# RWKV's short products in pairs: heads on rows or columns of the array, parities alternating

## The chip, the cores and the metric

The kernel runs on one core of a Trainium2 chip. The metric is the device time of one execution in microseconds, the median over several runs. A profile is one further execution, taken with the hardware profiler; its own time stands beside its span in the table below.

The engines are named as the profile names them: PE multiplies matrices (PEld is its loading of the stationary operand, the weights), DVE is the vector engine, ACT the scalar engine, POOL the general one, SP issues most transfers. PE writes to PSUM, which has eight banks; a tile of 128 partitions by 512 float32 fills one bank. DVE and ACT read the results out of it.

## The reference, cut to what matters

One decoder layer: a norm, one input projection, three mixers side by side (latent attention, RWKV-7, gated linear attention), a gated merge and an output projection, for 2048 tokens of width 1024. The change touches RWKV-7 alone, 8 heads of width 64:

```
def step(state, inp):
    r_t, w_t, k_t, v_t, kk_t, a_t = inp
    sa = jnp.einsum('bhvk,bhk->bhv', state, -kk_t)
    state = (state * w_t[:, :, None, :] + sa[..., None] * (kk_t * a_t)[:, :, None, :]
             + v_t[..., None] * k_t[:, :, None, :])
    return state, jnp.einsum('bhvk,bhk->bhv', state, r_t)
```

Each head has a 64 x 64 state that decays, is corrected and is read once a token. The kernel works it out in chunks of 64 tokens: inside a chunk the token-by-token dependence becomes a triangular system, and only the state passes from chunk to chunk. Decay and learning rate come from two low-rank products (`tanh(lw) @ w_up`, `la @ a_up`), each with an inner width of 64.

## The kernel before, in words

`phase_rwkv` walks 2048 tokens in four blocks of 512 (TB). For each block and each of two groups `g` of four heads (two pairs `q`, each pair with heads `hd` 0 and 1 on partitions 0-63 and 64-127), it projects r, k and v with weights split in two parts (`mm3`, L130-L135: three products of 128 x 128 weights by 512 tokens). Every projection product is full size; these are the "fill" below. A block-and-group is done as two halves `u` of 256 tokens, that is 16 pieces `i`, and a piece has four chunks `cc` of 64 tokens: `j = cc // 2`, parity `e_ = cc % 2`.

A piece goes through five steps, whose products are short:

- `operands` (L627) makes the scaled vectors `ar` (128 columns a chunk: 64 of r, 64 of a) and `bk` (64 of k, 64 of b), and the decays. Its two low-rank products (`tanh_up`, L645) use a `wup` that is padded with zeros to 128 rows, so that one half of the input is ignored.
- `within` (L408) makes the scores inside a chunk. `arb` is a block-diagonal copy of `ar` (head 0 in one half, head 1 in the other, zeros elsewhere; copied by POOL at L416 and ACT at L417), so that one product of 128 x 128 by 256 (L423) gives both heads. DVE masks the result into `ma` and `mr` (L426, L427).
- `inverses` and `whole` solve the triangular systems: DVE on 32 x 32 blocks, then 32 products of 32 x 32 in L478 and 32 in L488 for each two pieces, first all of one parity, then all of the other.
- `prepare` (L496) turns `bk` and makes `rv`: 16 products of 64 x 64 (L515), again one parity after the other.
- `chain` (L523) runs the four chunks one after another. The state of both heads of a pair is a block-diagonal 128 x 128 matrix `Zb` (its scales `scm` and `s0m` are masked by head on POOL). For each chunk: read the state (L556, two products of 128 x 128 by 128), add `rv` on DVE (L561), four products of 64 x 64 with the inverse (L565), copy to `uv` on ACT (L569), two products of 128 x 128 by 128 for the update (L575), add and scale on DVE (L580, L530). The output of the chunk before is read with four products of 128 rows by 64 columns (L547) and added on DVE (L549).

The program is not written in the order in which it runs: a scheduler lays out each engine's instructions beforehand, by priorities (`high_priority`) and its own model of durations, and each engine then runs its list in order. `place` ties the first product of each chain step to a point among the fill products, spread evenly over the piece. RWKV has these PSUM banks: one for each of `psm` (within), `ps1`, `psq`, `psa`, `psu`, `psz` and two for the projections.

After RWKV come the attention, the gated linear attention and the merge; they are untouched in the source. `[128*64]` in a profile row means 128 rows and 64 columns of the array. A float32 product stands in the profile as two passes, so counts there are twice the number of products in the source.

## Time and profile before

| what | value |
|---|---|
| median of 3 runs | 3022.0 us (3018.12 to 3023.85) |
| the profiled execution's own time | 3010.5 us |
| its span, first to last instruction | 3008.7 us |
| mean granted clock of PE | 0.989 |
| PE busy | 2908.3 us, 97% of the span |
| DVE, ACT, POOL busy | 59%, 50%, 49% |
| last RWKV short product starts | 1231.8 us |

A row of a group reads: line, engine, operation, what it writes and reads, shape and count, then busy time and the mean length of one in ns, then the idle time just before it and who ended it. A matmul's length includes its way through the array, and the next one starts before it ends; what one costs in a stream is the distance from start to start.

### The profile page before, as it was taken

The page shows a single profiled execution, that of the slowest core. Times are in us where ns is not written, and L with a number is a line of the kernel's source. Part 1 is how long each engine was busy: PE and PEld are TensorE (multiplying, and loading weights), DVE is VectorE, ACT ScalarE, POOL GpSimd, SP SyncE. Part 2 cuts the span into 40 slices and gives each one's busy share as a digit, 9 for nine tenths or more (in the row PEclk, how much of TensorE's full clock was granted, in tenths as well). Part 3 has the DMA queues.
Part 4 walks back from the last instruction along what each step waited for, and adds up shares of the span by engine and source line. Part 5 has one row for each costly group of instructions (what it writes and reads, how often), then busy time and mean ns, then how long its engine had stood idle before and what let it go on. Part 6 is the DMA issues. An engine that isn't in the chain of part 4 may idle for free. (4 is left out here: it accounts for less than half of the span.)

```text
span 3008.7 us, 52742 instructions
## 1 busy us (share of the span) xinstructions
PE 2908.3 (97%) x17728; PEld 2395.9 (80%) x17728; DVE 1761.0 (59%) x4677; ACT 1503.9 (50%) x3463; POOL 1474.7 (49%) x1945
## 2 busy tenths in 40 slices
PE   7998999999999999999999999999999999999998
PEld 6776777777777878789999887788788888778887
DVE  3558675667746544388888886744324312975443
ACT  4444434454444436577877775554334434554221
POOL 4644544454444435555544555776334424575322
PEclk9999999999999999999999999999999999999999
DMA  4333323323233334300000014444223226866422
GB/s 135 105 100 103 90 85 101 93 77 86 78 106 86 106 112 144 113 20 22 19 20 16 15 62 148 148 143 136 92 96 101 92 91 203 288 201 212 137 97 78
DMA packets 285184, 312.67 MB, mean 104 GB/s; under 512 B 77920, under 2 KB 234608, under 8 KB 284912
## 3 DMA queue, kind: packets, MB, share of 16 engines
q1 hardware_dynamic: 259088, 278.76, 29.3%
q10 hardware_dynamic: 25824, 30.54, 3.1%
q8 instruction: 140, 2.29, 0.3%
q14 instruction: 132, 1.08, 0.1%
HBM read 233.16 MB, written 76.02 MB: 103 GB/s over the span
## 5 line engine op out<-in xcount | busy, mean ns | idle before, releaser
L119 POOL TENSOR_TENSOR w_lo<-w_raw,w_hi 128x256 fp32r<-128x256 f32 x848 | 645.0, 768 | 818.9 <-ACT w_hi L118 770.6
L133 PE MATMUL psd<-hh,w_hi 128*128 128x512 f32 x1952 | 795.1, 408 | 10.7 <-ACT w_hi L118 4.2
L135 PE MATMUL psd<-hh,w_lo 128*128 128x512 f32 x1952 | 788.4, 406 | 9.2 <-POOL w_lo L119 8.7
L134 PE MATMUL psd<-hl,w_hi 128*128 128x512 f32 x1952 | 778.3, 399 | 0.0
L118 ACT CAST w_hi<-w_raw 128x256 fp32r<-128x256 f32 x848 | 336.4, 404 | 501.8 <-PE psd L134 281.9
L135 PEld LDWEIGHTS psd<-hh,w_lo 128*128 128x128 f32 x1952 | 371.4, 190 | 95.5 <-POOL w_lo L119 17.9
L133 PEld LDWEIGHTS psd<-hh,w_hi 128*128 128x128 f32 x1952 | 371.2, 190 | 91.7 <-issue 8.9
L134 PEld LDWEIGHTS psd<-hl,w_hi 128*128 128x128 f32 x1952 | 371.1, 190 | 74.8 <-issue 1.2
L1286 POOL TENSOR_SCALAR P<-P,nm 128x1024 f32<-128x1024 f32 (+2 forms) x192 | 166.1, 875 | 192.5 <-DVE nm L1283 144.6
L1306 DVE TENSOR_TENSOR tl<-pst,th 128x512 fp32r<-128x512 f32 (+2 forms) x352 | 193.4, 562 | 33.6 <-ACT th L1305 32.0
L1305 ACT CAST th<-pst 128x512 fp32r<-128x512 f32 (+2 forms) x352 | 165.2, 488 | 81.6 <-PE pst L1301 42.5
L1278 ACT ACTIVATE P<-P,nm 128x1024 f32<-128x1024 f32 (+2 forms) x192 | 172.3, 901 | 14.8 <-DVE nm L1274 14.5
L1264 DVE TENSOR_SCALAR_CACHE_REDUCE P<-pss 128x512 f32<-128x512 f32 (+3 forms) x288 | 168.2, 593 | 13.1 <-PE pss L135 9.5
L1301 PE MATMUL pst<-cs,P 128*128 128x128 f32 x1088 | 166.0, 274 | 0.0
L1323 PE MATMUL pso<-th,v 128*128 128x256 f32 x576 | 150.9, 284 | 2.6 <-DVE yo L1331 2.6
L1323 PE MATMUL pso<-tl,v 128*64 128x256 f32 x576 | 139.9, 282 | 0.7 <-DVE tl L1306 0.7
L1301 PEld LDWEIGHTS pst<-cs,P 128*128 128x128 f32 x1088 | 125.6, 141 | 9.1 <-DVE tl L1306 0.4
L133 PE MATMUL pss<-kh,qh 128*128 128x512 f32 (+2 forms) x320 | 128.7, 402 | 0.6 <-DVE mx L1268 0.2
L119 POOL TENSOR_TENSOR wb_lo<-wb_raw,wb_hi 128x256 fp32r<-128x256 f32 x96 | 87.8, 921 | 80.6 <-ACT wb_hi L118 65.4
L1323 PEld LDWEIGHTS pso<-th,v 128*128 128x128 f32 x576 | 108.8, 189 | 11.8 <-DVE yo L1331 2.8
L135 PE MATMUL pss<-kh,ql 128*128 128x512 f32 (+2 forms) x320 | 116.4, 365 | 0.6 <-POOL ql L1244 0.6
L134 PE MATMUL pss<-kl,qh 128*128 128x512 f32 (+2 forms) x320 | 116.3, 364 | 0.0
(403 smaller groups left out, 5925.2 us busy)
## 6 DMA issues: line engine op xcount, KB each, us to landing
w_raw<-in_w_gate_dram SPq DMA_DIRECT2D x448, 128.0 KB, 2.2
pre<-plain SPq DMA_DIRECT2D x144, 256.0 KB, 2.3
w_raw<-in_w_rwkv_dram SPq DMA_DIRECT2D x208, 128.0 KB, 2.2
w_raw<-in_w_more_dram SPq DMA_DIRECT2D x192, 128.0 KB, 2.2
h_g<-pre SPq DMA_DIRECT2D x48, 512.0 KB, 4.4
h_x<-in_x_dram SPq DMA_DIRECT2D x44, 512.0 KB, 4.5
more<-plain SPq DMA_DIRECT2D x48, 256.0 KB, 2.7
wb_raw<-in_w_br_dram ACTq DMA_DIRECT2D x96, 128.0 KB, 3.5
```

Of the source, the lines that this page charges most:

```text
L118: nc.scalar.copy(hi, src)
L119: (sub or nc.gpsimd).tensor_tensor(out=lo, in0=src, in1=hi.bitcast(F32), op=ALU.subtract)
L133: mm(out, lhsT=lhs[0], rhs=rhs[0], start=start, stop=False)
L134: mm(out, lhsT=lhs[0], rhs=rhs[1], start=False, stop=False)
L135: m = mm(out, lhsT=lhs[1], rhs=rhs[0], start=False, stop=stop)
L1264: nc.vector.tensor_scalar(out=pt[:, c0:c0 + f], in0=s_[:, 0:f], scalar1=-MLA_SCALE, scalar2=3e38, op0=ALU.mult, op1=ALU.min, accum_out=mx[ ...
L1278: nc.scalar.activation(out=pt[:, cw], in_=pt[:, cw], func=AF.Exp, bias=nm[:, 0:1], scale=-1.0, accum_out=nm[:, 1 + n:2 + n])
L1286: nc.gpsimd.tensor_scalar(out=pt[:, cw], in0=pt[:, cw], scalar1=nm[:, 1:2], scalar2=1.0, op0=ALU.mult, op1=ALU.mult)
L1301: nc.tensor.transpose(tp[:, kl, qt, :], P[qt][:, kt * 128:(kt + 1) * 128], k.ident)
L1305: nc.scalar.copy(flat(th)[:, r], flat(tp)[:, r])
L1306: nc.vector.tensor_tensor(out=flat(tl)[:, r], in0=flat(tp)[:, r], in1=flat(th)[:, r].bitcast(F32), op=ALU.subtract)
L1323: nc.tensor.matmul(d_, lhsT=l_, rhs=r_, start=kt == 0 and j == 0, stop=last and kl == 1 and j == 1)
```

## The change

The five steps compute the same, but no longer through block-diagonal copies. Each product that took both heads at once, with zeros in half of its operand, becomes two products that use a part of the array each, issued one right after the other:

- by rows (64 rows, 128 columns; head 0 on partitions 0-63, head 1 on 64-127, results to two different banks): the scores of `within` (L418 in the new numbering), the state read (L542), the two low-rank products (L639, now before both tanh).
- by columns (128 rows, 64 columns; results to partitions 0-63 and 64-127): the state update (L561) and the output read (L574), which is now done once for two chunks, both parities in turn.
- the products with the inverse (L551) stay 64 x 64, but the two heads go to different columns of the same rows. ACT copies the result in two halves instead of one.
- parities alternate product by product in L477, L487 (32 x 32) and L514 (64 x 64).

Gone are `arb` and its copies, `scm`, `s0m`, the zeros of `wup`. The state is 64 wide rather than 128, so DVE's add and scale handle half the elements. `psm` takes two banks, and `psa`, `psu`, `psz` are one two-bank tile `cz` that is made once. `psm` also takes the low-rank products and no longer helps in the first transposition.

```diff
-        ps_a = pool("rw_psa", 1, space=PSUM)
-        ps_u = pool("rw_psu", 1, space=PSUM)
-        ps_z = pool("rw_psz", 1, space=PSUM)
+        ps_c = pool("rw_psc", 1, space=PSUM)
...
+        cz = ps_c.tile([128, 2, 512], F32, name="psc")
+        pA = cz[:, :, 0:128].rearrange("p h (q v) -> p q h v", q=2)
+        pU, pZ, pY = cz[:, 0, 128:256], cz[:, 0, 384:512].rearrange("p (q v) -> p q v", q=2), cz[:, 1, 128:384]
...
             for q in range(2):
-                nc.gpsimd.tensor_copy(arb[0:64, :, 0, :], ar[0:64, q])
-                nc.scalar.copy(arb[64:128, :, 1, :], ar[64:128, q])
+                pm = ps_m.tile([128, 2, 512], F32, name="psm")
+                pv = pm.rearrange("p h (e j t) -> p e j h t", e=2, j=2)
+                for e_ in range(2):
+                    for j in range(2):
+                        for hd, hs in heads:
+                            nc.tensor.matmul(pv[:, e_, j, hd], lhsT=bk[hs, q, 2 * j + e_, :], rhs=ar[hs, q, 2 * j + e_, :],
+                                             start=True, stop=True)
...
-            for e_, (lo_, up_) in enumerate(half_):
-                for u in range(2):
-                    for n_ in range(8):
+            for u in range(2):
+                for n_ in range(8):
+                    for e_, (lo_, up_) in enumerate(half_):
                         m = nc.tensor.matmul(ph[up_, u, n_, :], lhsT=mas[u][lo_, e_, n_, 32:64], rhs=xh[lo_, u, n_, :],
...
-                for q in range(2):
-                    m = nc.tensor.matmul(pA[:, q * 128:(q + 1) * 128], lhsT=ar[:, q, cc, :], rhs=Zb[:, q, :],
-                                         start=True, stop=True)
...
+                    for hd, hs in heads:
+                        m = nc.tensor.matmul(pA[:, q, hd], lhsT=ar[hs, q, cc, :], rhs=Z[hs, q, :], start=True, stop=True)
...
+                for q in range(2):
+                    for hd, osl in enumerate((asl, rsl)):
+                        hc = slice((2 * q + hd) * 64, (2 * q + hd) * 64 + 64)
+                        m = nc.tensor.matmul(pU[osl, q * 64:q * 64 + 64], lhsT=T[asl, idx(q, hd, j), :], rhs=rhs[asl, hc],
+                                             start=True, stop=True)
...
+                for hd, osl in enumerate((asl, rsl)):
+                    nc.scalar.copy(by_head(uv[:, j, e_, :])[asl, :, hd], pU[osl].rearrange("p (q v) -> p q v", q=2))
...
+                        m = nc.tensor.matmul(pZ[hs, q, :], lhsT=bkt[:, q, cc, hs], rhs=uv[:, j, e_, hc],
+                                             start=True, stop=True)
...
+                if e_:
+
+                    for hn in range(4):
+                        hc = slice(hn * 64, hn * 64 + 64)
+                        for x in range(2):
+                            nc.tensor.matmul(pY[halves(x)[1], hc], lhsT=mr[:, x, idx(hn // 2, hn % 2, j), :],
+                                             rhs=uv[:, j, x, hc], start=True, stop=True)
+                    nc.vector.tensor_tensor(out=ysb[:, j, :], in0=pY, in1=ysb[:, j, :], op=ALU.add)
...
+            pw = ps_m.tile([128, 2, 512], F32, name="psm")
+            for q, p in enumerate(P2):
+                for r_, rs_ in heads:
+                    nc.tensor.matmul(pw[:, r_, q * 256:q * 256 + 256], lhsT=wup[rs_, p * 128:(p + 1) * 128],
+                                     rhs=lwla[rs_, ts_], start=True, stop=True)
```

Where the short products stand in PE's list follows from the scheduler. This is PE before, in the middle of the RWKV stage (L645 low-rank, L565 inverse, L423 scores, L547 output read; L133 to L135 and L601 are full-size fill and transposes):

```order
L645 MATMUL ps_8168<-lwla,wup 128x256 x2
L134 MATMUL psd_8754<-hl_8072,w_hi 128x512
...
L601 MATMUL psq<-cs,ysb 128x128 x4
L565 MATMUL psu<-rhs,tt_161 64x64 x4
L423 MATMUL psm<-arb,bk_7673 128x256 x2
L645 MATMUL ps_8194<-lwla,wup 128x256 x2
L547 MATMUL psu<-uv_6265,mr_6752 64x64 x4
```

Only the runs of L565 and L547 use a part of the array here; L423 and L645 use all of it, like the fill. This is PE of the change, at a place with the same kinds (L561 update, L514 `rv`, L418 scores, L542 state read):

```order
L135 MATMUL psd_11143<-hh_8054,w_lo 128x512
L561 MATMUL psc<-uv_8147,bkt 64x64 x4
L514 MATMUL psq<-uv_9167,ma_9955 64x64 x16
L418 MATMUL psm<-ar_10852,bk_10853 128x128 x5
L542 MATMUL psc<-z_149,ar_8144 128x64 x4
L418 MATMUL psm<-ar_10852,bk_10853 128x128 x3
L133 MATMUL psd_11195<-hh_8040,w_hi 128x512
```

Between the two fill products every run is now on a part of the array: 128 x 64, then 64 x 64, then 64 x 128 three times. The scores are eight half products instead of four runs of two, and another step's four stand inside them.

The low-rank products (L639) are issued as four in a row in most pieces, but not in all of them. PE of the change, in an early piece:

```order
L616 MATMUL ps_3306<-cs,sq 128x2
L639 MATMUL psm<-lwla,wup 128x256
L135 MATMUL psd_3141<-hh_2202,w_lo 128x512
L133 MATMUL psd_3141<-hh_2204,w_hi 128x512
...
L134 MATMUL psd_3196<-hl_2195,w_hi 128x512
L639 MATMUL psm<-lwla,wup 128x256
L135 MATMUL psd_3196<-hh_2194,w_lo 128x512
```

Here two products of a pair stand apart, each alone among full-size ones. Of the 64 low-rank products nine stand alone so; forty stand in runs of four. Counted over the whole list, the stretches of PE's list with one shape of the array are 361 before and 613 now.

More of the change, by code (lines that the diff above doesn't have):

```diff
@@ L376, in phase_rwkv @@
             nc.gpsimd.memset(tt[i], 0.0)
-        arb = per.tile([128, 4, 2, 128], F32, name="arb")
-        nc.gpsimd.memset(arb, 0.0)
         ones2 = k.c("ones2", 128)
@@ L560, in chain @@
                 rhs = t3.tile([128, 256], F32, name="rhs")
-                nc.vector.tensor_tensor(out=rhs[asl], in0=pA[asl], in1=rv[asl, j, :], op=ALU.add)
-                pU = ps_u.tile([128, 2, 256], F32, name="psu")
-                for hn in range(4):
-                    hc = slice(hn * 64, hn * 64 + 64)
-                    m = nc.tensor.matmul(pU[asl, 0, hc], lhsT=T[asl, idx(hn // 2, hn % 2, j), :], rhs=rhs[asl, hc],
-                                         start=True, stop=True)
-                    if hn == 0:
-                        at(m, 3 * cc + 1)
@@ L569, in chain @@
-                nc.scalar.copy(uv[asl, j, e_, :], pU[asl, 0])
-                nc.scalar.copy(ysb[rsl, j, :], pA[rsl])
-                if cc:
-                    read(cc - 1, pU)
-                pZ = ps_z.tile([128, 2, 128], F32, name="psz")
-                for q in range(2):
-                    m = nc.tensor.matmul(pZ[:, q, :], lhsT=bkt[:, q, cc, :], rhs=uv[:, j, e_, q * 128:(q + 1) * 128],
-                                         start=True, stop=True)
-                    if q == 0:
-                        at(m, 3 * cc + 2)
@@ L579, in chain @@
-                zt = t3.tile([128, 2, 128], F32, name="zt") if cc < 3 else Zb
-                nc.vector.tensor_tensor(out=zt, in0=pZ, in1=Zb, op=ALU.add)
-                if cc < 3:
-                    scaled(zt, scm[:, :, cc])
-            read(3, ps_u.tile([128, 2, 256], F32, name="psu"))
+                nc.vector.tensor_tensor(out=by_head(rhs)[asl], in0=pA[asl], in1=by_head(rv[:, j, :])[asl], op=ALU.add)
+                for q in range(2):
+                    for hd, osl in enumerate((asl, rsl)):
+                        hc = slice((2 * q + hd) * 64, (2 * q + hd) * 64 + 64)
+                        m = nc.tensor.matmul(pU[osl, q * 64:q * 64 + 64], lhsT=T[asl, idx(q, hd, j), :], rhs=rhs[asl, hc],
+                                             start=True, stop=True)
+                        if q == hd == 0:
+                            at(m, 3 * cc + 1)
@@ new lines, in chain @@
+                zt = t3.tile([128, 2, 64], F32, name="zt") if cc < 3 else Z
+                nc.vector.tensor_tensor(out=zt, in0=pZ, in1=Z, op=ALU.add)
+                if cc < 3:
+                    scaled(zt, sc[:, :, cc:cc + 1])
+                if e_:
+                    for hn in range(4):
+                        hc = slice(hn * 64, hn * 64 + 64)
+                        for x in range(2):
+                            nc.tensor.matmul(pY[halves(x)[1], hc], lhsT=mr[:, x, idx(hn // 2, hn % 2, j), :],
+                                             rhs=uv[:, j, x, hc], start=True, stop=True)
+                    nc.vector.tensor_tensor(out=ysb[:, j, :], in0=pY, in1=ysb[:, j, :], op=ALU.add)
@@ L640, in operands, with tanh_up @@
             P2 = (2 * g, 2 * g + 1)
[L642 to L650 removed]
+            pw = ps_m.tile([128, 2, 512], F32, name="psm")
[3 more added lines that the diff above has]
+                                     rhs=lwla[rs_, ts_], start=True, stop=True)
+            def tanh_up(r_):
+                o = t1.tile([128, 2, 256], F32, name="ta", bufs=2)
+                for q, p in enumerate(P2):
+                    nc.scalar.activation(out=o[:, q, :], in_=pw[:, r_, q * 256:q * 256 + 256], func=AF.Tanh,
+                                         bias=half[:, 4 * r_ + p:4 * r_ + p + 1], scale=0.5)
                 return o
[L654 removed]
+            ta, tb = tanh_up(0), tanh_up(1)
             ld = t1.tile([128, 8, 65], F32, name="ld")
@@ L734, in operands @@
                 nc.scalar.copy(uv[es, :, e_, :], pv[es].rearrange("p j q t -> p j (q t)"))
[L735 removed]
+            return dict(B=B, g=g, u=u, ar=ar, bk=bk, bv=bv, uv=uv, sc=sc, s0=s0)
         n = 4 * NB
@@ L811, in phase_rwkv @@
         k.more_constants()
-        wup = t1.tile([128, 2, 512], F32, name="wup")
-        nc.gpsimd.memset(wup, 0.0)
-        for r_ in range(2):
-            rows_ = slice(64 * r_, 64 * r_ + 64)
-            nc.scalar.dma_start(out=wup[rows_, r_], in_=w_up2[rows_])
-        blk["h"] = turned(xs, (pl.ps[1], "psd1"), (ps_1, "ps1"), (ps_m, "psm"), (ps_q, "psq"))
+        wup = t1.tile([128, 512], F32, name="wup")
+        nc.scalar.dma_start(out=wup, in_=w_up2)
+        blk["h"] = turned(xs, (pl.ps[1], "psd1"), (ps_1, "ps1"), (ps_q, "psq"))
         project_group(0)
```

91 lines of the change are left out of this document (29 added, 62 removed).

## The prediction

> **What bounds the kernel now.** I read the page first, then the stretches of the program, then PE's waits, then PE's timeline inside the RWKV stage.
>
> ```profile
> PE 2908.3 (97%) x17728; PEld 2395.9 (80%) x17728; DVE 1761.0 (59%) x4677; ACT 1503.9 (50%) x3463; POOL 1474.7 (49%) x1945
> ```
> ```profile
> 0.00:1235.00 1235.00, 1172.38 (x7334) 938.14 (x7335) 732.23 (x1902) 578.57 (x1377) 599.15 (x849) 0.98 0.34 101
> 1235.00:2000.00 765.00, 748.46 (x4971) 653.99 (x4971) 577.82 (x1889) 531.15 (x1226) 423.95 (x536) 0.99 0.19 60
> ```
> ```profile
> L547 PE MATMUL psu<-uv,mr x512: 221/222/368, 217.3 to 1231.8; 128*64 128x64 f32 x171
> ```
> ```profile
> PE psd L223 <- DVE h_x L202: 13.4, 2, 11.0
> PE psa L556 <- DVE zbd L530: 8.4, 7, 3.3
> PE psz L575 <- ACT uv L569: 2.5, 1, 2.5
> ```
>
> PE is busy for 97%, no other engine for more than 59%. The RWKV stage runs to 1235 us (its last short product starts at 1231.8), and PE works for 1172 of these. Its waits there are small: 13.4 us at the start, 8.4 us in all for the scaled state, 2.5 us for `uv`. So the stage takes what PE's list takes, and the change is to be priced on PE; DVE at 732, ACT at 579 and POOL at 599 us of 1235 have room. These are the short products, by group (two passes each; busy, mean ns of one):
>
> ```profile
> L423 PE MATMUL psm<-arb,bk 128*128 128x256 f32 x256 | 68.7, 388 | 0.4 <-DVE bk L715 0.4
> L547 PE MATMUL psu<-uv,mr 128*64 128x64 f32 x512 | 46.0, 230 | 0.0
> L575 PE MATMUL psz<-uv,bkt 128*128 128x128 f32 x256 | 45.4, 300 | 2.5 <-ACT uv L569 2.5
> L565 PE MATMUL psu<-rhs,tt 64*64 64x64 f32 x512 | 44.2, 225 | 2.7 <-DVE rhs L561 2.6
> L556 PE MATMUL psa<-zbd,ar 128*128 128x128 f32 x256 | 43.5, 294 | 10.8 <-DVE zbd L530 8.4 <-DVE gn_t L166 2.4
> L645 PE MATMUL ps<-lwla,wup 128*128 128x256 f32 x128 | 33.9, 387 | 0.7 <-ACT ta L649 0.4 <-DVE kl_v L161 0.3
> L515 PE MATMUL psq<-uv,ma 64*64 64x64 f32 x512 | 32.4, 222 | 0.4 <-ACT bkt L506 0.4
> L488 PE MATMUL psq<-tt,xt 32*32 32x32 f32 x512 | 19.0, 192 | 0.0
> L478 PE MATMUL psq<-xt,ma 32*32 32x32 f32 x512 | 18.9, 195 | 3.3 <-DVE xt L474 3.3
> ```
>
> Their lengths overlap, so I price a pass by its distance from start to start. Timeline rows (start, length of the run, count):
>
> ```profile
> 564.31 0.40 PE L135 MATMUL psd<-hh,w_lo 128*128 128x512 f32 x1
> 564.63 0.68 PE L565 MATMUL psu<-rhs,tt 64*64 64x64 f32 x8
> 565.24 0.51 PE L133 MATMUL psd<-hh,w_hi 128*128 128x512 f32 x1
> 565.58 0.40 PE L134 MATMUL psd<-hl,w_hi 128*128 128x512 f32 x1
> 565.81 0.40 PE L135 MATMUL psd<-hh,w_lo 128*128 128x512 f32 x1
> ...
> 573.75 1.03 PE L645 MATMUL ps<-lwla,wup 128*128 128x256 f32 x4
> ...
> 576.26 1.60 PE L478 MATMUL psq<-xt,ma 32*32 32x32 f32 x48 [0.20 <-DVE xt L474]
> 577.79 1.18 PE L556 MATMUL psa<-zbd,ar 128*128 128x128 f32 x4
> ...
> 586.57 0.71 PE L556 MATMUL psa<-zbd,ar 128*128 128x128 f32 x4
> 587.03 0.48 PE L133 MATMUL psd<-hh,w_hi 128*128 128x512 f32 x1
> ```
> ```profile
> 600.01 0.45 PE L515 MATMUL psq<-uv,ma 64*64 64x64 f32 x5
> ```
> ```profile
> 600.48 0.45 PE L515 MATMUL psq<-uv,ma 64*64 64x64 f32 x8
> ```
> ```profile
> 576.31 0.41 PE L478 MATMUL psq<-xt,ma 32*32 32x32 f32 x8
> ```
>
> - 64 columns: five L515 passes in 0.45 us, the last 0.22 long: 0.23 / 4 = 0.058 us a pass. 32 columns: (0.41 - 0.19) / 7 = 0.031.
> - 256 columns: (1.03 - 0.387) / 3 = 0.215. 128 columns: 587.03 - 586.57 = 0.46 for four, 0.115.
> - A round into a smaller shape of the array and back: from 564.31 to 565.58 stand two fill products (565.81 - 565.58 = 0.23 each) and eight passes, 0.46 + 0.46. They took 1.27, so **the round costs 0.35 us**.
>
> The Trainium skill, "TensorEngine Tiling (Array Packing)", section "Tiling Modes", says that a change of tiling mode drains the engine, and lists 64 rows by 128 columns as a mode. By it all row pairs pay, as in my sum; the 0.35 us agrees for 64 x 64, and no row here has 64 x 128.
>
> **Do pairs overlap?** The trace has two cases. At 600.48, where L515 passes from one parity to the other, and so to other rows and columns, eight passes stand in the stretch that holds five elsewhere. And the gated linear attention runs four column tiles:
>
> ```profile
> 1860.02 0.32 PE L1086 MATMUL psc<-qk 128*32 128x64 f32 x8 [1.16 <-DVE qk L1063]
> ```
>
> Eight passes of 64 columns with all starts within 0.32 - 0.22 = 0.10 us, where seven distances of 0.058 would be 0.41: four tiles run side by side. So two tiles give a factor k between 8/5 = 1.6 (the change-over, only part of which overlaps) and 2; I take 1.8.
>
> **Weights set a floor for the state read.**
>
> ```profile
> 150.21 0.61 PE L623 MATMUL ps<-cs,sq 128*128 128x2 f32 x4 [0.55 <-ACT sq L620]
> 150.68 0.48 PE L135 MATMUL psd<-hh,w_lo 128*128 128x512 f32 x1
> ```
>
> Four passes of only two columns took 0.47 us, as long as four of 128: a pass with weights of 128 columns costs 0.115 however little it multiplies. L542 halves the streamed columns, not the weights, and has twice the passes.
>
> **The sum.** PE before, in us: L565, L547, L515 each 512 x 0.058 = 29.7; L478 and L488 1024 x 0.031 = 31.7; L556 and L575 each 256 x 0.115 = 29.4; L423 256 x 0.215 = 55.0; L645 128 x 0.215 = 27.5. Together 262.
>
> After, were nothing side by side: inverse, output read, `rv` and update 4 x 29.7 (the update's weights now have 64 columns) = 118.8; 32 x 32 31.7; state read 512 x 0.115 = 58.9; scores 512 x 0.115 = 58.9; low-rank 27.5. Together 296, and 296 / 1.8 = 164. That is 98 less; with k = 1.6 it is 77, with k = 2 it is 114. Ten low-rank products whose partner stands elsewhere keep their full length: 20 x 0.215 / 2 = 2 back.
>
> Rounds: the stretches of one shape go from 361 to 613, 126 rounds more, x 0.35 = 44 back. The state read alone gives nothing (58.9 / 2 against 29.4) and pays 64 rounds; the update saves at most 14.5 and pays 64 rounds; scores, low-rank, inverse, `rv`, 32 x 32 and the halved number of output reads bring the gain. Bounds for a round that has no row, 64 x 128: nothing or 0.35; I take 0.35, the row of the other small shapes.
>
> The clock: the mean of the stage is 0.98, that is some 49 us at half speed, 25 us lost. The run of 32 x 32 passes before 577.79 is followed by such a stretch (L556 takes 1.18 us there, 0.71 at 586.57). With these runs half as long, I count 6 us less lost; bounds 0 and 25.
>
> The other engines:
>
> ```profile
> L569 ACT COPY uv<-psu 64x256 f32<-64x256 f32 x64 | 23.4, 366 | 17.7 <-PE psu L565 16.8
> L118 ACT CAST lh<-cl 128x128 fp32r<-128x128 f32 x48 | 13.3, 298 | 5.7 <-DVE cl L891 5.3
> L416 POOL COPY arb<-ar 64x512 f32<-64x512 f32 x32 | 23.4, 731 | 3.6 <-PE psm L423 2.6 <-DVE ar L713 0.9
> L426 DVE TENSOR_TENSOR ma<-psm,cs 128x256 f32<-128x256 f32 x64 | 26.9, 420 | 46.8 <-PE psm L423 46.6
> ```
>
> ACT copies `uv` twice: 2 x 0.30 (nearest row, 128 elements) for 0.37, 0.23 us more in 64 chunk steps. The update waits behind it, the DVE add behind the update, the next state read behind that. Chain steps are spread over a piece: 1235 / 16 = 77 us, 15 points, 5 us of fill between two; this hides it. Without that cover it is 64 x 0.23 = 15 us. The copies to `arb`, the masked scales and half of the elements in the state's add fall away, which PE did not wait for: nothing. One bank fewer in the first transposition lies beside the 13.4 us wait for the input: nothing; at worst two copies of about 0.7, 1.4 us. The order of fill in later stages is laid out anew; their products are the same, so I count zero and ten to either side.
>
> Sum: -98 + 2 + 44 - 6 = **-58 us**. From the profiled execution's 3010.5 (span 3008.7 and 1.8 around it) that is 2952.5. That execution lies 11.5 below the median of the three runs, 3022.0, so on the median's scale **2964 us**. With k from 1.6 to 2, the clock's bounds and the cover of `uv`, its own range is 2930 to 2995.
>
> **Rivals.** A change within 0.2%, 6 us, cannot be told from none.
>
> 1. *The row shape costs no round.* About 120 of the new stretches are 64 x 128; without 0.35 us each it is 42 us less: 2922. For it: no row shows the shape. Against it: all three smaller shapes that the trace has (64 x 64, 128 x 64, 32 x 32) are entered with the same gap after the fill. 12%.
> 2. *Pairs on the same rows don't overlap*, since weights for the second wait until the first has passed through these rows. It hits inverse, update and output read: 89.1 x (1 - 1/1.8) = 40 back, 3004. Against it speaks L1086, four tiles on the same 128 rows; for it, that those have 32 columns and no pair of 64 is in the trace. 10%. The Trainium skill states this rule, "TensorE: Matmul & The Clock Gate", "Part 3: Packing small matmuls": weights are loaded under a running product only when its row group differs; the trace disagrees for 32 columns.
> 3. *Pairs by rows don't overlap.* State read, scores and low-rank stay serial: 145.3 x (1 - 1/1.8) = 65 back, 3029, slower by a hair. For it: only the change-over of L515, where columns differ too, shows two row halves at work. Against: the heads' results go to two banks, so nothing that they write is shared. 10%.
> 4. *Waits on the one `psm`.* The second half of the scores must wait for four masks of the first (4 x 0.42 = 1.7 us), and the low-rank products now wait for the same tile. Exposed, 32 + 16 times 1.7 is 82 us: 3046, slower. It decides where fewer than seven fill products (7 x 0.23 = 1.6) stand between two users; PE's list mostly has more, and before, each half waited for two masks twice without showing (L423 idle before: 0.4 us). 6%.
> 5. *Nothing comes of it*: the scheduler's new order of the fill gives back what the pairs save. 4%.
>
> **How the numbers follow.** My forecast 58%, the rivals 12, 10, 10, 6 and 4. Faster by over 0.2%: 58 + 12 + most of 10, less the forecast's far tail, 0.79. Slower: rival 4 and two thirds of 3, 0.13. The rest, 0.08, is the same. The range for 8 in 10 takes in the forecast and rivals 1 and 2: 2916 to 3014; it leaves out 3, 4 and 5.
>
> **What would show it.** In the new profile, runs of L551, L561, L574 of eight, eight and sixteen passes should last about half of what their passes took serially; L418 (16 passes) about 1.0 us from its first start to its last rather than 1.7; L542 no shorter than L556 was, plus the gaps at its ends. L514 and the 32 x 32 runs should halve for certain. The end of the stage should move from 1232 to about 1175 us, the later stages keep their length. Serial starts in L561 speak for rival 2, in L418 for rival 3, PE waits on DVE's masks at L418 for rival 4. The forecast is wrong if the stage shortens by under 15 us, or by over 100.

## The result, and the profile after

The changed kernel takes 2985.2 us in the median of 4 runs (2984.7 to 2988.2), the kernel before 3020.1 beside it (3011.1 to 3023.9): a ratio of 0.9892, 95% interval 0.9876 to 0.9908, 35 us less. The forecast was 58 us less, 2964. Two further groups of runs of the same program (they stand among the experiments) gave 2986.8 and 2985.0.

The views that the prediction began with, for the changed kernel: the page's first row, the stretches of the RWKV stage and of what follows (columns: length, then PE, PEld, DVE, ACT, POOL busy, the granted clock, the share of the DMA engines, GB/s), and the record of the output read (L574; its counterpart L547 started last at 1231.8 us before); then span and clock of both kernels.

```profile
PE 2861.1 (96%) x18496; PEld 2309.9 (77%) x18496; DVE 1718.7 (58%) x4642; ACT 1493.3 (50%) x3495; POOL 1444.3 (48%) x1865
```
```profile
0.00:1235.00 1235.00, 1158.74 (x8280) 880.47 (x8280) 694.40 (x1876) 580.86 (x1442) 580.78 (x787) 0.97 0.36 104
1235.00:2000.00 765.00, 740.77 (x5004) 647.34 (x5005) 583.91 (x1905) 534.93 (x1237) 431.99 (x550) 0.98 0.20 61
```
```profile
L574 PE MATMUL psc<-uv,mr x512: 222/222/368, 211.8 to 1231.6; 128*64 128x64 f32 x171
```
```profile
core 0: 3008.7 us, clock 0.989
```
```profile
core 0: 2983.6 us, clock 0.982
```

Three things are not as forecast. The last short product still starts at 1231.6 us: the recurrence has not moved, although the pairs are shorter. The granted clock fell, from 0.989 to 0.982 over the whole execution. The clock records of the traces hold only full and half clock. At half clock for a share s of the span, the mean clock is 1 - s / 2, so (1 - clock) x span is what the half clock costs while PE has work: 33 us before, 54 us after. And PE's idle time, the span less what PE is busy, rose from 100 us (3008.7 - 2908.3) to 122 (2983.6 - 2861.1). Nearly all of it came in the RWKV stage and at its end, first before, then after:

```profile
0.00:1200.00 1200.00, 1137.38 (x7138) 910.56 (x7139) 718.01 (x1871) 555.62 (x1314) 577.91 (x815) 0.98 0.34 100
1200.00:1300.00 100.00, 98.29 (x534) 79.66 (x533) 44.76 (x155) 58.61 (x151) 56.04 (x78) 1.00 0.30 96
```
```profile
0.00:1200.00 1200.00, 1127.21 (x8051) 855.92 (x8052) 678.67 (x1840) 562.85 (x1389) 567.54 (x765) 0.97 0.36 105
1200.00:1300.00 100.00, 87.09 (x541) 71.75 (x542) 61.80 (x219) 58.39 (x144) 46.96 (x60) 0.90 0.15 45
```

PE is idle for 10 us more up to 1200 us, and for 11 more in the 100 us behind that. So the two traces can be taken apart. The cost of the half clock is an estimate: half of the time for which PE was busy at half clock (59 us before, 90 after, by the clock records).

| part of the span, us | before | after | change |
|---|---|---|---|
| PE idle | 100 | 122 | +22 |
| half clock while PE is busy | 29 | 45 | +16 |
| the rest, PE's work | 2879 | 2816 | -63 |
| span | 3008.7 | 2983.6 | -25 |

(The traced execution of the kernel before was some 10 us faster than its median, so the traces differ by 25 us where the medians differ by 35.)

**The pairs themselves.** PE's timeline around a state read, first before, then after (start, length of the run, count):

```profile
683.24 0.40 PE L134 MATMUL psd<-hl,w_hi 128*128 128x512 f32 x1
683.47 0.61 PE L556 MATMUL psa<-zbd,ar 128*128 128x128 f32 x4
683.84 0.47 PE L135 MATMUL psd<-hh,w_lo 128*128 128x512 f32 x1
684.15 0.39 PE L133 MATMUL psd<-hh,w_hi 128*128 128x512 f32 x1
```
```profile
931.02 0.39 PE L133 MATMUL psd<-hh,w_hi 128*128 128x512 f32 x1
931.34 0.66 PE L542 MATMUL psc<-z,ar 64*128 64x64 f32 x8
931.93 0.50 PE L134 MATMUL psd<-hl,w_hi 128*128 128x512 f32 x1
932.27 0.39 PE L135 MATMUL psd<-hh,w_lo 128*128 128x512 f32 x1
```

From the fill product ahead to the second one behind it took 0.91 us before and 1.25 after; two fill products are 0.46 of that, so a state read costs 0.45 us before and 0.79 after. That is near the loss that the prediction's sum held (four passes of 0.115, against eight in pairs and a round of 0.35). The eight passes lie within 0.66 us, and a pass takes 0.27, so all starts fall within 0.39, where seven serial distances of 0.115 would be 0.80: row pairs overlap. The same reading for the other stretches, where fill stands on both sides, and what the prediction's figures give for each with its k of 1.8:

| stretch | before, us | after, us | times | change | predicted |
|---|---|---|---|---|---|
| state read | 0.45 | 0.79 | 64 | +22 | +26 |
| update | 0.46 | 0.58 | 64 | +8 | +10 |
| inverse | 0.80 | 0.58 | 64 | -15 | -13 |
| output read | 0.80 x 64 | 0.81 x 32 | | -25 | -24 |
| scores | 0.87 x 64 | 1.30 x 32 | | -14 | -11 |

(Before, some output reads stood right behind another short run and shared its round, so -25 is an upper bound.) From start to start, with waits and half clock included, rv goes from 30 to 18 us, the 32 x 32 products from 36 to 26, the low-rank products from 27 to 21.5. Together that is about 52 us, where the prediction had -98 + 2 + 44 = -52. It is an estimate: only 29 of the 64 state reads before, and 35 after, stand alone between two fill products as in the rows above. The work in the two whole traces fell by 63 us (table above). The column pairs overlap like the row pairs. The Trainium skill, "TensorE: Matmul & The Clock Gate", "Part 3: Packing small matmuls", lets weights load under a running product only for another row group. The runs of L561, on 128 rows with two column halves, contradict it: in the run that starts at 1095.31 us, weights begin to load at 1095.36 while the products that began at 1095.31 on the same rows run on to 1095.58, and eight passes take 0.45 us where L565 took 0.68 for eight on one tile. The measurement decides.

**The end of the stage.** Stretches of 20 us, before and then after, and the two waits that stand in PE's timeline there:

```profile
1220.00:1240.00 20.00, 20.00 (x107) 15.81 (x106) 9.99 (x24) 10.95 (x30) 11.52 (x19) 1.00 0.37 119
1240.00:1260.00 20.00, 19.57 (x87) 15.42 (x87) 1.46 (x5) 6.88 (x17) 10.38 (x14) 1.00 0.45 148
```
```profile
1220.00:1240.00 20.00, 12.38 (x112) 10.37 (x113) 9.45 (x30) 6.04 (x18) 3.11 (x6) 0.87 0.04 14
1240.00:1260.00 20.00, 15.13 (x59) 11.82 (x58) 8.87 (x38) 9.16 (x22) 10.76 (x12) 0.62 0.15 47
```
```profile
1239.24 1.12 PE L594 MATMUL psq<-cs,ysb 128*128 128x128 f32 x4 [7.39 <-POOL ysb L590]
1247.60 0.45 PE L133 MATMUL pss<-kh,qh 128*128 128x128 f32 x1 [4.68 <-issue]
```

The fill is done before the recurrence is. In the trace of before, 131 fill products start behind the last output read; in the trace of after none does. So PE waits for the chain's last operations (7.39 us for the normalised output) and for the attention's first operands, and drops to half clock: 0.87 and 0.62. Behind that, the stages keep their lengths.

**Waits and the half clock.** By the clock records, half clock takes 48 us before and 72 after up to 1200 us, none and 20 in the next 100, and 21 and 15 in the rest of the span. In the middle of the stage, much shorter waits than 7.39 us stand ahead of it. A row of PE's timeline after, and the two stretches of 3.41 us around the point where the clock changes:

```profile
530.69 0.45 PE L561 MATMUL psc<-uv,bkt 128*64 128x64 f32 x8 [2.00 <-ACT ysb L557]
```
```profile
528.19:531.60 3.41, 1.41 (x13) 0.86 (x12) 3.38 (x17) 1.97 (x6) 0.58 (x1) 1.00 0.13 39
531.60:535.01 3.41, 3.41 (x9) 2.54 (x8) 3.41 (x12) 1.29 (x3) 2.60 (x4) 0.50 0.12 38
```

PE was idle for 2.00 of 3.41 us, and the next 3.41 us ran at half clock. In the traces every half-clock stretch starts on a grid of 3.41 us. Of the grid's full-clock steps behind the first 60 us, in the traces of before, of the parities alone (below) and of after together, 23 had PE idle for 2 us or more, and all 23 were followed by half clock; of 2336 with less than 0.5 us idle, one was; of 148 between, 15 were.

### The profile page after: what moved, and what is told of

It is laid out like the page before. It is cut to its first block, busy times and chain, and to the rows that moved or that the text cites. A ratio compares the mean times of both kernels' runs of the same rounds, so it can differ in the third digit from the quotient of the medians.

```text
span 2983.6 us, 54189 instructions
## 1 busy us (share of the span) xinstructions
PE 2861.1 (96%) x18496; PEld 2309.9 (77%) x18496; DVE 1718.7 (58%) x4642; ACT 1493.3 (50%) x3495; POOL 1444.3 (48%) x1865
## 4 chain that ended last, share of the span: by engine, by line
PE 65%; DVE 9%; DMA 3%; ACT 2%; issue 2%; POOL 1%; SPq 0%; ACTq 0%; DVEq 0%; POOLq 0%
PE psd L133 10%; PE psd L135 10%; PE psd L134 10%; PE pso L1307 4%; PE pst L1285 4%; PE pss L133 3%; PE pss L135 3%; PE pss L134 3%; PE psb L135 2%; PE psg L133 2%; PE psg L135 2%; PE psg L134 2%; PE psb L133 2%; PE psb L134 2%; PE psc L1070 1%
## 5 line engine op out<-in xcount | busy, mean ns | idle before, releaser
L133 PE MATMUL psd<-hh,w_hi 128*128 128x512 f32 x1952 | 798.7, 410 | 16.9 <-DVE carry L402 6.6
L135 PE MATMUL psd<-hh,w_lo 128*128 128x512 f32 x1952 | 787.5, 405 | 9.1 <-POOL w_lo L119 8.7
L133 PEld LDWEIGHTS psd<-hh,w_hi 128*128 128x128 f32 x1952 | 372.4, 191 | 109.1 <-ACT w_hi L118 17.1
L135 PEld LDWEIGHTS psd<-hh,w_lo 128*128 128x128 f32 x1952 | 372.5, 191 | 100.4 <-POOL w_lo L119 18.6
L133 PE MATMUL pss<-kh,qh 128*128 128x512 f32 (+2 forms) x320 | 129.3, 404 | 5.1 <-issue 4.7
L135 PE MATMUL pss<-kh,ql 128*128 128x512 f32 (+2 forms) x320 | 117.0, 367 | 0.1
```

The source lines that it names most:

```text
L133: mm(out, lhsT=lhs[0], rhs=rhs[0], start=start, stop=False)
L135: m = mm(out, lhsT=lhs[1], rhs=rhs[0], start=False, stop=stop)
```

## The experiments

The numbers of all runs. "Clock" is the mean over the timed executions; "lost" is (1 - clock) x span; "rest" is the time without it. Half-clock time in which PE waited anyway is counted as lost too, so "lost" is an upper bound; "rest" holds PE's waits as well as its work. For "again" the clock is the profile's, since one of its six executions (3003.0 us) read 0.928. The kernel before has a clock of 0.988 in its 23 runs of one group: 38 us lost, rest 2981.

| kernel | median, us | before beside it | ratio (95%) | clock | lost | rest |
|---|---|---|---|---|---|---|
| the changed kernel | 2985.2 | 3020.1 | 0.9892 (0.9876 to 0.9908) | 0.982 | 54 | 2931 |
| again | 2986.8 | 3018.4 | 0.9902 (0.9882 to 0.9922) | 0.982 (profile) | 54 | 2933 |
| parities alone | 2989.4 | 3018.6 | 0.9912 (0.9897 to 0.9927) | 0.991 | 26 | 2964 |
| row pairs apart | 3002.2 | 3018.6 | 0.9953 (0.9935 to 0.9970) | 0.982 | 54 | 2948 |
| all pairs apart | 3004.0 | 3018.6 | 0.9958 (0.9946 to 0.9970) | 0.985 | 45 | 2960 |
| state read full | 2984.7 | 3018.4 | 0.9890 (0.9873 to 0.9907) | 0.983 | 51 | 2934 |
| state read and update full | 2962.6 | 3015.4 | 0.9829 (0.9808 to 0.9851) | 0.987 | 39 | 2924 |
| fill held back | 2991.4 | 3015.4 | 0.9924 (0.9905 to 0.9942) | 0.981 | 57 | 2934 |
| both | 2972.5 | 3015.4 | 0.9859 (0.9839 to 0.9879) | 0.988 | 37 | 2935 |
| both, held gently | 2973.7 | 3018.1 | 0.9861 (0.9841 to 0.9881) | 0.987 | 40 | 2934 |

I set out with a theory (A): the pairs work, but the chain steps keep their place in time, and the gain is lost where the fill ends too early. Its rival (B): PE's list and its clock set the time, and the end of the stage gives nothing back.

### One part alone: the parities

```diff
-            for e_, (lo_, up_) in enumerate(half_):
-                for u in range(2):
-                    for n_ in range(8):
+            for u in range(2):
+                for n_ in range(8):
+                    for e_, (lo_, up_) in enumerate(half_):
```

This in the kernel before, for both loops of 32 x 32 products, and the same in the loop of `rv`; nothing else.

> The kernel before, in which only the loops of the 32 x 32 products and of the inverse's right-hand products (rv) let the parities alternate: no new stretch, no new round, no other operation. The prediction's sum gives (29.7 + 31.7) x (1 - 1/1.8) = 27 less; the start-to-start distances of the two traces give 22 less (rv 30 to 18, 32 x 32 36 to 26). Theory A (a gain is lost only where the fill ends before the chain; the kernel before has some 23 us of fill behind its chain): all of it shows, 20 to 27 less. Theory D (the scheduler's order gives back what pairs save, wherever it is saved): under 10 less.

It took 2989.4 us, 29 less than the kernel before. The three groups that it changes (busy, mean ns, idle before; the kernel before had 32.4, 18.9 and 19.0 us), then its span and clock:

```profile
L515 PE MATMUL psq<-uv,ma 64*64 64x64 f32 x512 | 20.8, 222 | 0.0
L478 PE MATMUL psq<-xt,ma 32*32 32x32 f32 x512 | 14.1, 202 | 5.8 <-DVE xt L474 5.6
L488 PE MATMUL psq<-tt,xt 32*32 32x32 f32 x512 | 13.0, 193 | 0.0
```
```profile
core 0: 2990.6 us, clock 0.990
```

The three groups are busy for 22 us less (70.3 to 47.9), and three changed loops give 29 us, a little above theory A's 20 to 27, where the whole change gives 32 to 35. The gain of the parities is not lost anywhere (theory D falls): 17 us of it are in the rest, 12 in the clock (0.988 to 0.991). All the other parts of the change together, which take some 30 us out of PE's list (+22 + 8 - 15 - 25 - 14 - 6), give only 3 to 6. In the table their work is there: the rest falls by another 33 us, from 2964 to 2931. But the clock falls to 0.982, and 28 us more are lost by it than with the parities alone. Taken apart as above, the two traces (2990.6 and 2983.6 us) say the same and add the waits: PE's work falls by 42 us, half clock while PE is busy costs 20 more (25 to 45), and PE is idle for 14 more (108 to 122). That is where the missing gain is.

### Pairs taken apart

```diff
-                for e_ in range(2):
-                    for j in range(2):
-                        for hd, hs in heads:
+                for hd, hs in heads:
+                    for e_ in range(2):
+                        for j in range(2):
                             nc.tensor.matmul(pv[:, e_, j, hd], ...
...
-                for q in range(2):
-                    for hd, hs in heads:
+                for hd, hs in heads:
+                    for q in range(2):
                         m = nc.tensor.matmul(pA[:, q, hd], ...
```

Both in the changed kernel, and likewise in the low-rank products: head after head.

> The changed kernel, with the row pairs taken apart: in the scores, the state read and the low-rank products all products of the first head are issued, then all of the second (same products, same shapes, same number of stretches). If row pairs overlap fully, PE has 512 x 0.115 + 512 x 0.115 + 27.5 = 145 us to do where the trace of the change shows 104, some 41 more (33 if the change-over between the heads still overlaps). Theory A: the first 18 of it fill the gap behind the fill, so that 15 to 25 us show: about 3005. Theory B (PE's list alone sets the end): 33 to 41, about 3022. If row pairs don't overlap (rival 3): none, 2985.

The second kernel does the same with the inverse, the update and the output read.

> As the one before, and the column pairs (inverse, update, output read) taken apart too. They take 26 + 27 + 27 = 80 us in pairs by the trace, 89 x (some 1.15 for the single gaps) serially where nothing overlaps: 119 - 10 or 20 for the output read, where two of four change-overs remain. If column pairs overlap: 25 to 35 us more than with the row pairs alone apart; now past the tail's slack, so nearly all of it shows: about 3035, slower than the kernel before. If they don't: no difference.

Measured: 3002.2 and 3004.0 us, 17 and 19 more than the changed kernel. PE's timeline of a run of each kind: first of the changed kernel, then with the row pairs apart, then with all pairs apart.

```profile
743.78 1.16 PE L418 MATMUL psm<-ar,bk 64*128 64x128 f32 x16
```
```profile
874.20 0.69 PE L574 MATMUL psc<-uv,mr 128*64 128x64 f32 x16
```
```profile
1095.31 0.45 PE L561 MATMUL psc<-uv,bkt 128*64 128x64 f32 x8
```
```profile
722.31 1.71 PE L418 MATMUL psm<-ar,bk 64*128 64x128 f32 x16
725.98 0.67 PE L542 MATMUL psc<-z,ar 64*128 64x64 f32 x8
```
```profile
1022.64 0.46 PE L561 MATMUL psc<-uv,bkt 128*64 128x64 f32 x8
1026.62 0.97 PE L574 MATMUL psc<-uv,mr 128*64 128x64 f32 x16
```

Runs of sixteen passes get longer: the scores 1.16 to 1.71 us (32 x 0.55 = 18), the output read 0.69 to 0.97 (32 x 0.28 = 9). Runs of eight do not: the state read takes 0.67 against 0.66, the update 0.46 against 0.45. There the second head's passes start beside the first's (the first of them 13 ns behind, against 6 ns in the changed kernel) although they are issued behind all four of them. In the runs of sixteen, by the spacing of the starts, the second head begins beside the fifth of the first head's eight passes, with three of them still to start. So the pairing by rows is real and worth what it was priced at in the scores, but in a run of eight the order of issue does not matter; my expectation of 33 to 41 us, or 25 to 35 for the columns, took every run as serial. The 18 us that the scores lost show in the time one for one (17), which speaks for theory B: work that is added to PE's list is paid (by the traces PE's work rises by 20 us, its idle time falls by 4). The output read's 9 us stand in the rest (2948 to 2960), and a higher clock gave them back.

### The state read on the full array again

```diff
+                for hd, hs in heads:
+                    nc.vector.tensor_tensor(out=Zb[hs, :, hd], in0=src[hs], in1=sc_[hs].broadcast_to([64, 2, 64]), op=ALU.mult)
-                nc.vector.tensor_tensor(out=Z, in0=src, in1=sc_.broadcast_to([128, 2, 64]), op=ALU.mult)
+                nc.gpsimd.tensor_tensor(out=Z, in0=src, in1=sc_.broadcast_to([128, 2, 64]), op=ALU.mult)
...
-                    for hd, hs in heads:
-                        m = nc.tensor.matmul(pA[:, q, hd], lhsT=ar[hs, q, cc, :], rhs=Z[hs, q, :], start=True, stop=True)
+                    m = nc.tensor.matmul(pA[:, q], lhsT=ar[:, q, cc, :], rhs=Zb[:, q].rearrange("p h v -> p (h v)"), start=True, stop=True)
```

> The changed kernel, but the state is read back as before: one full 128 x 128 product for two heads on a block-diagonal copy of the state (two DVE operations of 64 partitions write it, POOL writes the compact state beside it). It takes 256 full-array passes for 512 passes in row pairs, and 64 stretches in a smaller shape fewer. By the prediction's sum (29.4 against 58.9 / 1.8 = 32.7, and 64 rounds x 0.35 = 22) PE has 22 to 26 us less to do; by the start-to-start distances of the two traces (33 against 42) some 9. Theory A (the end of the stage hangs on the chain's place, not on PE's sum): little of that shows here, 0 to 8 us less than the changed kernel. Theory B (PE's list alone sets the end): 9 to 26 less. A loss of over 5 us would say that the additional DVE operations or POOL's copy stand in the chain's way.

2984.7 us, no gain, although PE's list is 64 x 0.34 = 22 us shorter. PE's waits up to 1300 us (us in all, times, the longest), of the changed kernel and then of this one:

```profile
PE psd L135 <- POOL w_lo L119: 7.8, 10, 4.0
PE psc L542 <- DVE z L529: 5.2, 4, 2.2
PE psc L551 <- DVE rhs L546: 3.5, 4, 1.3
```
```profile
PE psd L135 <- POOL w_lo L119: 12.7, 10, 4.0
PE psc L554 <- DVE rhs L549: 10.0, 7, 4.6
PE psc L545 <- DVE zbd L532: 6.2, 6, 3.0
```

The fill's weights wait 5 us longer for POOL, the inverse 6.5 longer for DVE's add: I had added one operation on DVE and one on POOL to every step of the recurrence. By the traces PE is busy for 19 us less (2861.1 to 2842.4) and idle for 12 more. So this run cannot tell A from B: its own additions may have eaten the gain. The next one has no such addition.

### State read and update on the full array

```diff
-                nc.vector.tensor_tensor(out=Z, in0=src, in1=sc_.broadcast_to([128, 2, 64]), op=ALU.mult)
+                nc.vector.tensor_tensor(out=Zb.rearrange("p q (h v) -> p q h v", h=2),
+                                        in0=src.rearrange("p q (h v) -> p q h v", h=2),
+                                        in1=sm.unsqueeze(3).broadcast_to([128, 2, 2, 64]), op=ALU.mult)
...
-                    for hd, hs in heads:
-                        m = nc.tensor.matmul(pA[:, q, hd], lhsT=ar[hs, q, cc, :], rhs=Z[hs, q, :], start=True, stop=True)
+                    m = nc.tensor.matmul(pA[:, q], lhsT=ar[:, q, cc, :], rhs=Zb[:, q, :], start=True, stop=True)
...
-                        m = nc.tensor.matmul(pZ[hs, q, :], lhsT=bkt[:, q, cc, hs], rhs=uv[:, j, e_, hc],
-                                             start=True, stop=True)
+                    m = nc.tensor.matmul(pZ[:, q, :], lhsT=bkt[:, q, cc, :], rhs=uv[:, j, e_, q * 128:(q + 1) * 128],
+                                         start=True, stop=True)
```

The two parts of the change that the prediction's sum held to be losses are undone (with the masked scales that belong to them); everything else stays in pairs.

> The changed kernel, with two of its parts undone: the state read and the update are full 128 x 128 products on a block-diagonal state again, with masked scales. Scores, inverse, output read, low-rank, rv and 32 x 32 products stay in pairs. By the lengths of whole stretches in the traces (state read 0.45 against 0.79 us, update 0.46 against 0.58, 64 of each) PE has 29 us less to do, and the recurrence has no more operations on DVE than before. Theory B (PE's list alone sets the end): 25 to 30 less than the changed kernel, about 2957. Theory A': 0 to 8 less, since the fill only runs further ahead.

2962.6 us, 53 less than the kernel before beside it and 23 less than the changed kernel: by the ratios 19 to 22 less. That is near theory B's 25 to 30, and not A's 0 to 8. This is the fastest kernel of the study, and it beats both.

```profile
core 0: 2957.8 us, clock 0.987
```

By the table, 15 us of the gain are clock (0.982 to 0.987) and 7 are the rest. The traces (2983.6 and 2957.8 us) agree: half clock while PE is busy costs 14 us less (45 to 31), PE's work falls by 10, its idle time by 1. So the 29 us that the list was to lose do not show: they were priced by runs that stand alone between fill products, and in the changed kernel only 35 of 64 state reads and 33 of 64 updates do. The number is near theory B's, but its mechanism, that PE's list alone sets the time, is not what these traces show. What is shown is the price of the two parts together, some 20 us.

### The end of the stage: an edit that moved nothing

```diff
-                fill = fill[:len(fill) // 2]
+                fill = fill[:len(fill) // 4]
```

> The changed kernel, in which only a quarter (not half) of the last fill is used to space the recurrence of the last two pieces, so that these chain steps stand earlier in the fill and products of the fill are left behind them. Same work. Theory A (the pairs made the fill end 43 us earlier, but the last chain steps keep their place in time, so that PE runs dry behind the fill for some 18 us, part of it at half clock): 15 to 20 us less than the changed kernel, about 2967. Theory B (the shortfall lies in the small stretches themselves, in rounds and clock, and the tail costs nothing that could be got back): no change, 2985. Theory C (chain steps packed closer wait on DVE and ACT): 5 to 15 us more.

> Both edits together: the full-array state read, and the last chain steps placed earlier in the last fill. Against the run with the earlier chain steps alone: 22 less if a round costs 0.35 us and a row pair of the state read gains nothing else, 9 less by the start-to-start distances, 0 if leaving and entering the row shape is free. Theory A expects the two gains to add up: 2945 to 2958.

> Control: the kernel before, with only a quarter (not half) of the last fill used to space the last two pieces' recurrence. Its fill reaches over the chain's end already. Theory A: no change, within 5 us. If it also gets some 15 us faster, the earlier chain steps help for another reason than a fill that the pairs made too short.

> The changed kernel as it is, beside the three that follow, as their yardstick. Expected: 0.989 of the kernel before, 33 us less, as measured first.

2985.0, 2985.6, 3019.9 and 2986.8 us. PE's order comes out the same with this edit as without it, in all three kernels: the points to which chain steps are tied are lower bounds, and none of them binds; the steps stand where the scheduler's own model of durations puts them. So the first three runs test nothing and are repeats. They show how well a number repeats: the same program gave 2985.2, 2986.8 and 2985.0, and 2984.7 and 2985.6.

### The end of the stage: fill held back

```diff
+        if self.hold is not None:
+            self.place(m0, [self.hold], 0)
...
-                    gates(NB - 1, blk["h"], range(N_SOON, w_gate.shape[0]))
+                    for n_ in range(N_SOON, w_gate.shape[0]):
+                        at_ = 156 + (n_ - 6) * 12 // 30
+                        k.hold = k.steps[at_] if at_ >= 0 else None
+                        gates(NB - 1, blk["h"], (n_,))
+                    k.hold = None
```

`m0` is a projection's first product, `k.steps` the first products of the chain's steps, 12 a piece.

> The changed kernel, in which the last fill of the RWKV stage (30 gate projections of the last block, 720 products) may no longer run ahead of the recurrence: each projection's products are ordered behind one of the 12 steps of the last piece but two (in PE's order, without a new wait). Same work. In PE's list 142 fill products now stand behind the last output read, where the changed kernel has none and the kernel before 131. Theory A' (what the pairs saved went into fill that ran ahead, because the recurrence stands in PE's list at the pace that the scheduler gave it, and PE then has nothing to do at the stage's end): 12 to 25 us less than the changed kernel, about 2967, and the 7.4 us wait for POOL and the half clock at the end of the stage go. Theory B (the end of the stage costs nothing that can be got back): no change, 2985. Theory C (the recurrence cannot go faster than it stands, so that PE waits on DVE and ACT between its steps): no change or slower, with waits on L529's and L546's results.

2991.4 us: 5 to 6 more than the changed kernel (7 to 10 by the ratios), not 12 to 25 less. (In the trace 150 fill products stand behind the last output read, not 142.) The stretches, of the changed kernel and then of this one:

```profile
900.00:1000.00 100.00, 97.63 (x739) 75.48 (x736) 56.18 (x159) 45.56 (x113) 50.70 (x66) 0.98 0.37 104
1000.00:1100.00 100.00, 98.38 (x758) 74.88 (x757) 40.01 (x117) 38.79 (x97) 39.74 (x53) 0.97 0.40 117
```
```profile
900.00:1000.00 100.00, 87.65 (x767) 68.31 (x765) 57.70 (x166) 40.84 (x100) 41.27 (x53) 0.91 0.30 83
1000.00:1100.00 100.00, 91.24 (x715) 70.28 (x717) 44.52 (x136) 40.13 (x103) 35.93 (x51) 0.93 0.37 108
...
1220.00:1240.00 20.00, 19.78 (x92) 15.88 (x91) 0.00 (x0) 6.82 (x16) 8.72 (x12) 1.00 0.37 120
1240.00:1260.00 20.00, 18.70 (x109) 15.15 (x109) 11.39 (x51) 11.26 (x30) 11.71 (x14) 1.00 0.10 33
```

The end is mended: PE busy 19.78 and 18.70 of 20 us, the clock at 1.00. The hole is now between 900 and 1100 us: 21 us idle there, where it was 4, and the clock at 0.91 and 0.93. Moving the fill moves the hole, and the half clock goes with it. Theory A falls as far as it said that the end could be mended at no price.

The same hold on the kernel with full state read and update, and a gentler one, with fewer projections held at a time:

> Both edits: state read and update full again, and the last fill held back behind the recurrence. In PE's list 122 fill products stand behind the last output read. Theory A' expects the whole of PE's saving to show here: 29 + 12 to 25 less than the changed kernel, 2931 to 2946. Theory B: as with the full products alone. Theory C: no better than with the full products alone, with new waits on DVE and ACT.

> The changed kernel with the full-array state read and update, and the last fill held back gently: in PE's list 117 and 90 fill products stand beside the third and second last piece (189 and 184 without the hold, 45 and 162 with the hard one), and 78 behind the last output read (none, and 122). The hard hold emptied 900 to 1010 us of the trace instead of the stage's end (PE busy 82 of 100 us there). Theory B' (the fill is short as a whole: wherever it is taken from, PE waits there instead, and drops to half clock there): no faster than without the hold, 2962 or up to 5 more. Theory A'' (some 100 products a piece are enough cover, so that the end is filled at no price): 8 to 15 less, about 2950. It also tries for a version that beats both kernels by more.

2972.5 and 2973.7 us, both 10 to 11 us slower than without a hold (by the ratios, 0.0030 and 0.0032 of 3018, 9 and 10 us). In the traces 136 and 84 fill products stand behind the last output read. The gentle hold:

```profile
900.00:1000.00 100.00, 90.86 (x711) 70.87 (x711) 54.45 (x151) 43.59 (x107) 44.95 (x62) 0.98 0.31 92
1000.00:1100.00 100.00, 89.25 (x666) 71.38 (x665) 42.35 (x139) 39.42 (x102) 34.31 (x50) 0.95 0.37 111
```

20 us idle between 900 and 1100, as with the hard hold on the changed kernel, and 7 without a hold. This fits a fill that is short as a whole: once the short products are faster, PE no longer has enough other work to put between the steps of the recurrence, and wherever a hole is left, PE waits and slows down in it. No run with more fill tests that.

## Why the prediction was right, and where it was off

**The direction and the mechanism were right.** Pairs by rows and by columns overlap; rivals 2 and 3 fall by the runs of L561 and L418. Rival 1 falls by the state read: of its 0.79 us, 0.39 lie between the first start and the last, which leaves 0.40 for entering and leaving the 64 x 128 shape; the prediction held 0.35. Rival 4 does not occur: PE lists no wait on a mask ahead of L418. Rival 5, that the order of the fill gives the gain back, was rated at 4% and holds in part: waits and half clock that came with the new order gave part of the gain back, as below.

**The sum over PE's list was near**: -52 predicted, about -52 by the stretches, -63 by the work in the whole traces. Within it k is nearer 2 than 1.8 for the pairs of L551, L561 and L542, but 1.7 for rv (30 to 18) and for the second loop of 32 x 32 products (L488 17.6, L487 10.3 us from start to start), which were to "halve for certain". The shares lie as said: state read and update are losses, parities, inverse, output read and scores bring the gain.

**Two terms failed, the clock and the waits.** On the clock the prediction says "I count 6 us less lost; bounds 0 and 25". It was some 16 us more (38 to 54), outside these bounds, and the sign was wrong. The waits it put at nothing ("this hides it", "the stage takes what PE's list takes"): PE's idle time rose by 22 us. With the right clock alone the sum would have been -98 + 2 + 44 + 16 = -36, and 35 were measured, but that is luck: the work fell by 11 us more than the sum, the waits took 22, and the traced execution before was 10 us faster than its median. I had tied the half clock to the runs of 32 x 32 passes alone. The parities' own run agrees with this part: with the shorter runs by themselves (rv among them) the clock rises to 0.991, 12 us less lost, more than the 6. But the rest of the change takes work from PE that had covered waits, and a wait costs twice, once for itself and once by the half clock behind it: at the end of the stage 7.39 us of wait up to 1239, then 0.62 in 1240 to 1260; in the middle 2.00 us of wait at 530.69, then 3.41 us at half clock. The Trainium skill, "TensorE: Matmul & The Clock Gate", "HAM oscillation — how this bites in real kernels", says that an idle gap of some 3.4 us halves the clock; the trace agrees at the end of the stage, with 7.39 us idle and 0.62 behind it, but in the middle 2 us within 3.41 were enough, and there the measurement decides. The hold shows the link of hole and clock, since both moved together, and the count over three traces shows it for the waits of 2 us and more; that waits cause all of the fall is not shown, since 16 of the 39 half-clock stretches counted there follow less idle time.

**"The end of the stage should move from 1232 to about 1175 us" was wrong.** It took the recurrence for a part of PE's list that moves up when the list gets shorter. The scheduler spaces its steps by its own model, and the freed time went into fill that runs ahead. The last output read stayed at 1231.6, the fill ended some 43 us earlier, and the first transposition of the attention moved from 1280.2 to 1255.7 us, by 25.

**The cover of `uv`, and "zero" for later stages**: the update waits for ACT for 2.4 us in all, in two places (the 2.00 us at 530.69 is one, put down to the copy of `ysb` behind the two of `uv`), and the stages behind RWKV kept their lengths to 3 us.

Partly open is why the clock falls by 0.009 between the parities alone and the whole change. By the two traces, half clock takes 20 us more at the end of the stage, where PE waits for 9 us more, and 24 us more before 1200 us, where PE's idle time rose by only 3 us (70 to 73). What makes the half clock longer there is not shown.

## What to carry to other kernels

Price each small product with the whole stretch it stands in, from one full-size neighbour to the next: a pair that halves the streamed columns but not the weights, as the state read does, only pays the change of shape. Where loops over independent parts of the array already exist, alternate them first; here that gave 29 of 32 to 35 us for three reordered loops. And where PE is the bound with little idle time, ask of every saving what covers the waits afterwards: when the cover gets short, waits appear, and those that leave PE idle for 2 us of 3.4 were paid a second time here, at half clock.

## What the runs showed of the hardware

- Two products on different parts of the array need not be issued next to each other. In runs of eight passes, four and four, they overlapped fully in either order (0.67 against 0.66 us, 0.46 against 0.45); in runs of sixteen, eight and eight, only in part (1.71 against 1.16, 0.97 against 0.69). So PE looks past passes that wait for their part of the array: in all these runs past three, by the starts; whether it can look further was not measured.
- Entering and leaving a 64 x 128 shape costs about as much as for 64 x 64: 0.40 us beside the 0.39 of the state read's starts, and 0.34 beside the 0.46 of L565's.
- The granted clock is a term of its own. Over ten kernels with the same work outside RWKV it lay between 0.981 and 0.991, which is 57 to 26 us of 3000: a spread of 31 us, nearly what the whole change gained.
- Idle time of 2 us within a step of 3.41 us was followed by half clock in 23 of 23 cases in three traces; with less than 0.5 us idle it was in 1 of 2336.
